# A two-layer recurrent trunk on one core: tokens halved in order instead of by parity

## The chip, the cores and the metric

The kernel runs on one core of a Trainium2 chip. Its engines are TensorE (matrix products, PE in the profile, with its weight loads shown apart as PEld), VectorE (DVE), ScalarE (ACT), GpSimd (POOL) and SyncE (SP), which here only issues transfers. The metric is the device time of one execution in microseconds; for the kernel before, the median of three runs is 1073.52 us.

## The reference

Two layers over 256 tokens of width 2048, all in fp32. The first layer projects the normed tokens into an HGRN2 mixer and an RG-LRU mixer, the second into an mLSTM mixer; each ends in an output projection added to the residual and in a gate that is a full 2048 x 2048 product:

```python
h = h + mix
pl = rmsnorm(p[i].astype(h.dtype) @ ple_w[i], ple_norm[i])
h = h + jax.nn.sigmoid(h @ ple_gate_w[i]) * pl
```

After the second layer a last RMSNorm is applied. What matters here is that each of the products takes all 256 tokens, that the output projections and gates produce rows by token (the residual is kept so), and that the next product needs these rows turned, features on the partitions.

## The kernel before

**Products.** Every operand is split into a rounded part and a remainder (hi and lo, type fp32r), and each product is made as hi·hi + hi·lo + lo·hi. `load_weights` (L116) brings 512 KB pieces through SyncE's queue into `raw` (five buffers), ACT casts them into `whi` (L130), VectorE subtracts into `wlo` (L131); both have four buffers, each a half of a quarter. `block` (L154) makes products with the weights stationary. `project_tok` (L190) makes those with the tokens stationary: for a block of 512 output columns it goes through four quarters `kq` of the contraction, in each through two halves of the tokens `hf`, and issues for each of four 128-row steps three products of 512 columns (L205, L206, L207): 96 products per column block, 24 per quarter. `quarter` (L1146) does the same with 256 columns for the last 512 output columns of the last gate.

**Which tokens form a half.** `tokens` (L187) picks the stationary operand. Where `even` is set, half 0 holds the even and half 1 the odd tokens: a step of two fp32 values over 128 columns. That is so in the output projections (`out_proj`, weights eo and oo), the gates (`ple_gate` with g0, and g1 with its last quarter) and the embeddings (`embed`). Elsewhere (ei, ez, ov, oog, oz) a half is 128 tokens in a row. The residual `hq` is loaded by parity (L882) and the result stored by parity (L1202).

**From rows to features.** After each column block c of an output projection or of g0, `to_features` (L353) turns 512 columns of the residual: VectorE transposes in blocks of 32 x 32 into w (L358), POOL writes w to DRAM (L476) and reads it back in four pieces as r (L479), and ACT and VectorE split r into the hi and lo of the next stationary operand. Without a gain (lanes fe after eo, fo after oo) ACT copies 256 columns (L370) and VectorE subtracts 256 (L371); with the gain of the next norm (lane fg after g0) `scaled_split` does both with a scale (L267, L268). In the lane fg a further step follows: `gate_sums` (L896), eight small products of r with the 16 columns of mLSTM's gates, with fp32 operands.

**Order.** Lanes are Python generators. `pump` (L74), called once in each quarter of a projection, takes every lane one `yield` further, behind the instructions last noted. `across` yields three times around the way through DRAM. `ready` (L376) lets the first projection of the next stage ask, at each quarter, for the two operands that this quarter needs; the last quarter needs the last column block of the stage before. Each engine takes its own queue in order; that order is fixed when the program is built, from the order of issue, `high_priority` and `issue_after`, and can differ from the order of the lines (the timeline shows two L205 behind each other where a lo part comes late).

**The norm ahead of the second layer.** `hidden_norm` (L909) sums squares, takes the reciprocal root per token, and spreads it along the free axis: a diagonal is built (L230), TensorE multiplies it with ones (L233), ACT copies the result (L251). Since its tokens are halved by parity and the following projections want halves in order, two more VectorE instructions (L917) pick the reordered values. ov's first eviction needs the values per token, the query and key projections the spread ones.

Of the kernel before, what the change touches and what calls it, by code (L numbers as in the profile page):

```python
# [19 lines left out]
P = 128  # L20
# [23 lines left out]
def trunk(ctx: ExitStack, tc: tile.TileContext, a, out):  # L44
# [142 lines left out]
    def tokens(x, k, hf, even):  # L187
        return x[:, k, hf::2] if even else x[:, k, hf * P:(hf + 1) * P]

    def project_tok(w, j, act, before=None, even=False):  # L190

        ps = [pm.tile([P, 512], F32, name="mm", tag="mm") for _ in range(2)]
        for kq in range(4):
            if before is not None:
                before(kq)
            parts = load_weights(w[4 * j + kq])
            for hf in range(2):
                for kk in range(4):
                    k = kq * 4 + kk
                    hi, lo = parts[kk // 2]  # L200
                    c = (kk % 2) * 512
                    ah, al, _ = act[k // 2]
                    xh, xl = (tokens(x, k % 2, hf, even) for x in (ah, al))
                    wh, wl = hi[:, c:c + 512], lo[:, c:c + 512]
                    te.matmul(ps[hf], xh, wh, start=(k == 0), stop=False)  # L205
                    te.matmul(ps[hf], xh, wl, start=False, stop=False)  # L206
                    last["pe"] = te.matmul(ps[hf], xl, wh, start=False, stop=(k == KT - 1)).ins  # L207
                if hf == 0:
                    pump()
        return ps  # L210
# [16 lines left out]
    def to_free(rt, even=False):  # L227

        dg = tp.tile([P, T], F32, name="dg", tag="dg", bufs=1)
        v.tensor_tensor(out=dg.rearrange("p (t h) -> p h t" if even else "p (h t) -> p h t", h=2), in0=ident.unsqueeze(1).to_broadcast([P, 2, P]),  # L230
                        in1=rt.unsqueeze(2).to_broadcast([P, 2, P]), op=ALU.mult)
        st = pst.tile([P, 512], F32, name="st", tag="st")
        te.matmul(st[:, 0:T], ones[:, 0:P], dg, start=True, stop=True)  # L233
        return st[:, 0:T]
# [13 lines left out]
    def free_copy(rt, name, even=False):  # L248
        ps = to_free(rt, even)
        rs = tp.tile([P, T], F32, name=name, tag="rsb")  # L250
        s.copy(rs, ps)  # L251
        return rs
# [45 lines left out]
    def embed(w, pact, tile_of, first=None):  # L298

        pls = []  # L300
        for b in range(2):
# [3 lines left out]
            for hi, lo in parts:  # L305
                halves = []
                for hf in range(2):
                    ps = pm.tile([P, 512], F32, name="mm", tag="mm")
                    for k in range(2):
                        xh, xl = (tokens(x, k, hf, True) for x in pact[0:2])  # L310
# [42 lines left out]
    def to_features(h, c, act, gain, name, more=None):  # L353

        w = room("w")
        w5 = w.rearrange("p (j c t h) -> p h c j t", j=4, c=4, h=2)
# [4 lines left out]
        r4 = r.rearrange("p (i c n) -> p c i n", i=4, c=4)  # L361
        for b in range(2):
            hi, lo, both = act_pair()
            for k in range(2):
                src = r4[:, 2 * b + k]
                hk, lk = (x[:, k].rearrange("p (i n) -> p i n", i=4) for x in (hi, lo))
                if gain:
                    scaled_split(src, gain, 4 * c + 2 * b + k, hk, lk)
                else:
                    s.copy(hk, src)  # L370
                    v.tensor_tensor(out=lk, in0=src, in1=hk.bitcast(F32), op=ALU.subtract)  # L371
            act[2 * c + b] = (hi, lo, both)
        if more is not None:
            more(c, r4)
# [8 lines left out]
    def out_proj(hq, w, y, lane):  # L383

        act = {}
        for c in range(4):
            ps = project_tok(w, c, y, even=True)
# [7 lines left out]
    def ple_gate(hq, w, act, pls, rp, hss, gain, lane, before, more):  # L395

        nxt = {}
        for c in range(4):
            ps = project_tok(w, c, act, None if c else before, even=True)
# [496 lines left out]
    def gate_sums(c, r4):  # L896
        for x in range(4):
            te.matmul(gps[32 * x:32 * x + 32, 0:T], wt[:, 4 * c + x], r4[:, x], start=(c == 0), stop=(c == 3))
# [10 lines left out]
    def hidden_norm():  # L909

        r = rsqrt_cols(total(hss0, 4))
        yield
        rs = free_copy(r, "hrs", even=True)
        rt, rth = (tp.tile([P, 2], F32, name=n, tag=n) for n in ("rt1", "rth"))
        for hf in range(2):
            sq = tp.tile([P, 512], F32, name="sq", tag="sq")[:, 0:P]
            v.scalar_tensor_tensor(sq, rs[:, hf * P:(hf + 1) * P], 1.0, ident, op0=ALU.mult, op1=ALU.mult,  # L917
                                   accum_out=rt[:, hf:hf + 1])
        v.tensor_scalar(rth, rt, 0.5, None, op0=ALU.mult)
        norm.update(rs=rs, rt=rt, rth=rth)  # L920
        yield
# [3 lines left out]
    with tc.tile_pool(name="m1", bufs=2) as m1:  # L925
# [212 lines left out]
        for g in range(3):  # L1138
            ps = project_tok(a["g1"], g, act, None if g else ready(act, "fo"), even=True)
# [6 lines left out]
        def quarter(g, order):  # L1146
            parts = load_weights(a["g1e"][2 * g]) + load_weights(a["g1e"][2 * g + 1])
            ps = [pm.tile([P, 512], F32, name="mm", tag="mm")[:, 0:T] for _ in range(2)]
            for n, (hf, kq) in enumerate(order):
                hi, lo = parts[kq]  # L1150
                for kk in range(4):
                    k = kq * 4 + kk
                    xh, xl = (tokens(x, k % 2, hf, True) for x in act[k // 2][0:2])
# [18 lines left out]
        for hf, ps in enumerate(quarter(1, [(hf, kq) for hf in range(2) for kq in range(4)])):  # L1172
# [15 lines left out]
            for g, c, n in ((1, 0, 256), (1, 256, 256), (0, 0, 512), (2, 0, 512), (3, 0, 512)):  # L1188
# [13 lines left out]
                x = on.dma_start(out=out.rearrange("(p h) f -> h p f", h=2)[hf, :, g * 512 + c:g * 512 + c + n], in_=o).ins  # L1202
# [119 lines left out]
```

## Time and profile before

| | us |
|---|---|
| median of three runs | 1073.52 |
| lowest and highest run | 1071.8, 1074.81 |
| the profiled execution | 1067.43 |
| its span, first to last instruction | 1065.7 |
| TensorE busy | 1049.1 |
| VectorE busy | 724.9 |
| ACT busy | 583.9 |

The stages with the tokens stationary lie in the profiled span at 308.7 to 397.6 us (eo), from there to some 492 us (g0), then ov up to 581 us, oog and oz up to 864 us, the second embedding, oo from 876.8 to 965.7 us, and g1 up to 1057 us with its last quarter from 1033.9 us. Rows of the profile name the line of the kernel, the engine, the operation and the tiles as out<-in; in a group's row the busy time and the mean duration of one follow, then the idle time ahead of them and what ended it. In the rows of a line stand the least, median and largest duration and the first and last start.

### The profile page before, as it was taken

What the parts mean: (1) busy time and instruction counts of PE and PEld (TensorE: products, weight loads), DVE (VectorE), ACT (ScalarE), POOL (GpSimd) and SP (SyncE); (2) the same over time, 40 slices, a digit from 0 to 9 for tenths busy, and PEclk for the clock granted to TensorE, in tenths of its full rate; (3) what the DMA queues carried; (4) which work ended last, traced back from release to release, by engine and by line L of the source; (5) the groups of instructions that cost most, each with busy time, mean ns of one, the idle gap of its engine ahead of it and who ended that gap; (6) DMA issues with size and microseconds to landing.
All of it is one profiled execution on the core that took longest, in us unless ns stands there. A gap on an engine that the chain in (4) does not pass through costs nothing.

```text
span 1065.7 us, 15134 instructions
## 1 busy us (share of the span) xinstructions
PE 1049.1 (98%) x5614; PEld 883.9 (83%) x5614; DVE 724.9 (68%) x1055; ACT 583.9 (55%) x877; POOL 143.4 (13%) x166
## 2 busy tenths in 40 slices
PE   7999999999999999999999999999999999999996
PEld 6888888888888888777888888888888888888886
DVE  6757797997876666657444887764457675656666
ACT  7675545869653444545445656654445575444543
POOL 0001332512204211111000000000001113311111
PEclk9999999999999999999999999999999999999998
DMA  9765554545868777766655544546557775877552
GB/s 358 276 215 189 173 166 151 178 159 191 262 249 257 238 230 219 237 218 228 201 187 196 173 159 159 168 159 197 198 185 233 250 260 184 274 241 234 193 178 80
DMA packets 63098, 221.21 MB, mean 208 GB/s; under 512 B 7728, under 2 KB 9008, under 8 KB 63024
## 3 DMA queue, kind: packets, MB, share of 16 engines
q1 hardware_dynamic: 55440, 196.64, 55.0%
q0 software_dynamic: 7152, 23.07, 7.2%
q8 instruction: 44, 0.72, 0.3%
q10 hardware_dynamic: 432, 0.52, 0.1%
q14 instruction: 30, 0.25, 0.1%
HBM read 209.20 MB, written 11.01 MB: 207 GB/s over the span
## 4 chain that ended last, share of the span: by engine, by line
PE 86%; issue 7%; DMA 4%; DVE 1%; POOL 1%; ACT 1%; ACTq 0%; POOLq 0%; DVEq 0%
PE mm L205 17%; PE mm L207 17%; PE mm L206 17%; PE mm L161 16%; PE mm L167 9%; DMA dfe<-w 2%; POOL r L479 1%; DMA dfg<-w 1%; PE mm L315 1%; PE mm L316 1%; PE mm L317 1%; PE mm L1157 1%; PE mm L1156 1%; PE mm L1155 1%; PE mx L792 1%
## 5 line engine op out<-in xcount | busy, mean ns | idle before, releaser
L131 DVE TENSOR_TENSOR wlo<-raw,whi 128x1024 fp32r<-128x1024 f32 (+1 forms) x363 | 443.4, 1237 | 261.0 <-ACT whi L130 227.3
L130 ACT CAST whi<-raw 128x1024 fp32r<-128x1024 f32 (+1 forms) x363 | 377.5, 1043 | 358.9 <-PE mm L207 262.3
L205 PE MATMUL mm<-whi,ahl 128*128 128x512 f32 x992 | 390.4, 394 | 0.0
L206 PE MATMUL mm<-wlo,ahl 128*128 128x512 f32 x992 | 388.5, 392 | 0.0
L207 PE MATMUL mm<-whi,ahl 128*128 128x512 f32 x992 | 387.9, 392 | 0.0
L205 PEld LDWEIGHTS mm<-whi,ahl 128*128 128x128 f32 x992 | 189.2, 191 | 39.5 <-ACT ahl L370 0.6
L207 PEld LDWEIGHTS mm<-whi,ahl 128*128 128x128 f32 x992 | 189.2, 191 | 39.4 <-issue 0.4
L206 PEld LDWEIGHTS mm<-wlo,ahl 128*128 128x128 f32 x992 | 189.3, 191 | 39.3 <-issue 0.8
L161 PE MATMUL mm<-ahl,whi 128*128 128x512 f32 x768 | 183.2, 391 | 0.0
L161 PEld LDWEIGHTS mm<-ahl,whi 128*128 128x128 f32 x768 | 141.4, 188 | 27.4
L167 PE MATMUL mm<-ahl,wlo 128*128 128x256 f32 x768 | 102.1, 286 | 0.0
L167 PEld LDWEIGHTS mm<-ahl,wlo 128*128 128x128 f32 x768 | 97.2, 191 | 3.6 <-issue 0.4
L476 POOL DMA_DIRECT2D ducn<-w x3 | 1.7, 561 | 332.7 <-DVE w L489 332.7
L173 ACT COPY sm<-mm 128x256 f32<-128x256 f32 x48 | 17.5, 365 | 30.9 <-PE mm L167 30.9
L938 DVE SCALAR_TENSOR_TENSOR qk<-mg,prm,qk 128x255 f32<-128x255 f32 (+2 forms) x48 | 21.1, 477 | 5.0 <-ACT qk L935 4.7
L174 DVE TENSOR_TENSOR mg<-mm,sm 128x256 f32<-128x256 f32 x48 | 19.9, 416 | 0.1
L315 PE MATMUL mm<-whi,ahl 128*128 128x512 f32 x32 | 14.1, 440 | 5.5 <-ACT whi L130 5.5
L1156 PE MATMUL mm<-wlo,ahl 128*128 128x256 f32 x64 | 18.1, 283 | 0.0
L1157 PE MATMUL mm<-whi,ahl 128*128 128x256 f32 x64 | 18.1, 283 | 0.0
L1155 PE MATMUL mm<-whi,ahl 128*128 128x256 f32 x64 | 18.1, 282 | 0.0
L184 DVE TENSOR_TENSOR mg<-mg,hrs 128x512 f32<-128x512 f32 (+1 forms) x25 | 17.1, 682 | 0.6
L358 DVE STREAM_TRANSPOSE w<-hq 128x512 f32<-128x512 f32 x24 | 17.0, 708 | 0.3
(288 smaller groups left out, 788.7 us busy)
## 6 DMA issues: line engine op xcount, KB each, us to landing
raw<-in_ew_dram SPq DMA_DIRECT2D x64, 512.0 KB, 4.2
raw<-in_g_dram SPq DMA_DIRECT2D x56, 512.0 KB, 4.4
raw<-in_eo_dram SPq DMA_DIRECT2D x32, 512.0 KB, 4.8
raw<-in_ov_dram SPq DMA_DIRECT2D x32, 512.0 KB, 3.8
raw<-in_oqk_dram SPq DMA_DIRECT2D x32, 512.0 KB, 4.0
raw<-in_oog_dram SPq DMA_DIRECT2D x32, 512.0 KB, 3.8
raw<-in_oz_dram SPq DMA_DIRECT2D x32, 512.0 KB, 3.9
raw<-in_oo_dram SPq DMA_DIRECT2D x32, 512.0 KB, 4.8
```

Source lines behind the costliest of these rows:

```text
L130: last["act"] = s.copy(h, r).ins
L131: last["dve"] = v.tensor_tensor(out=l, in0=r, in1=h.bitcast(F32), op=ALU.subtract).ins
L161: last["pe"] = te.matmul(ps, parts[k // 8][0][:, c:c + P], act[k // 2][2][:, (k % 2) * 512:(k % 2 + 1) * 512], start=(k == 0), stop=False).ins
L167: last["pe"] = te.matmul(ps[:, T:2 * T], parts[k // 8][1][:, c:c + P], act[k // 2][0][:, k % 2], start=False, stop=(k == KT - 1)).ins
L205: te.matmul(ps[hf], xh, wh, start=(k == 0), stop=False)
L206: te.matmul(ps[hf], xh, wl, start=False, stop=False)
L207: last["pe"] = te.matmul(ps[hf], xl, wh, start=False, stop=(k == KT - 1)).ins
L315: te.matmul(ps, xh, wh, start=(k == 0), stop=False)
L938: v.scalar_tensor_tensor(dst[:, sh:T], pi[:, 0:T - sh], pc("ccw", k * 16 + b), dst[:, sh:T], op0=ALU.mult, op1=ALU.add)
L1155: te.matmul(ps[hf], xh, wh, start=(k == 0), stop=False)
L1156: te.matmul(ps[hf], xh, wl, start=False, stop=False)
L1157: last["pe"] = te.matmul(ps[hf], xl, wh, start=False, stop=(k == KT - 1)).ins
```

## The change

Every half of the tokens is now 128 tokens in a row, and the parameter `even` is gone. The residual is loaded and the result stored in that order. The transposes write w in the order of halves. When r is split, the tokens are put in order: without a gain the copy and the subtractions go through a pattern with the halves outermost, the subtraction in two pieces of 128 columns; with a gain ACT writes scaled columns in order into a new tile x, and `split_act` makes hi (a copy of 512 columns) and lo (a subtraction of 512 columns) from it. The small gate products come two yields after the split. The norm ahead of the second layer uses `spread_norm`, one yield later at its start and one more ahead of the spreading, and the two reordering instructions are gone.

```diff
-    def tokens(x, k, hf, even):
-        return x[:, k, hf::2] if even else x[:, k, hf * P:(hf + 1) * P]
+    def tokens(x, k, hf):
+        return x[:, k, hf * P:(hf + 1) * P]
...
-        w5 = w.rearrange("p (j c t h) -> p h c j t", j=4, c=4, h=2)
+        w5 = w.rearrange("p (j c h t) -> p h c j t", j=4, c=4, h=2)
...
-        r4 = r.rearrange("p (i c n) -> p c i n", i=4, c=4)
+        r5 = r.rearrange("p (i c h t) -> p c h i t", i=4, c=4, h=2)
         for b in range(2):
-            hi, lo, both = act_pair()
-            for k in range(2):
-                src = r4[:, 2 * b + k]
-                hk, lk = (x[:, k].rearrange("p (i n) -> p i n", i=4) for x in (hi, lo))
-                if gain:
-                    scaled_split(src, gain, 4 * c + 2 * b + k, hk, lk)
-                else:
+            if gain:
+                x = tp.tile([P, 512], F32, name="xr", tag="hn", bufs=3)
+                for k in range(2):
+                    s.activation(x[:, k * T:(k + 1) * T].rearrange("p (h i t) -> p h i t", h=2, i=4), r5[:, 2 * b + k],
+                                 AF.Copy, scale=pc(gain, 4 * c + 2 * b + k))
+                act[2 * c + b] = split_act(x, "h")
+            else:
+                hi, lo, both = act_pair()
+                for k in range(2):
+                    src = r5[:, 2 * b + k]
+                    hk, lk = (x[:, k].rearrange("p (h i t) -> p h i t", h=2, i=4) for x in (hi, lo))
                     s.copy(hk, src)
-                    v.tensor_tensor(out=lk, in0=src, in1=hk.bitcast(F32), op=ALU.subtract)
-            act[2 * c + b] = (hi, lo, both)
+                    for hf in range(2):
+                        v.tensor_tensor(out=lk[:, hf], in0=src[:, hf], in1=hk[:, hf].bitcast(F32), op=ALU.subtract)
+                act[2 * c + b] = (hi, lo, both)
         if more is not None:
-            more(c, r4)
+            yield
+            yield
+            more(c, r5)
...
-    def spread_norm(rt):
+    def spread_norm(rt, lag=0):
         norm["rt"] = rt
         yield
+        if lag:
+            yield
         norm["rs"] = free_copy(norm["rt"], "hrs")
...
-            gp.dma_start(out=t, in_=a["x"].rearrange("(p h) f -> p h f", h=2)[:, :, i * 512:(i + 1) * 512])
+            gp.dma_start(out=t, in_=a["x"].rearrange("(h p) f -> p h f", h=2)[:, :, i * 512:(i + 1) * 512])
...
-    def gate_sums(c, r4):
+    def gate_sums(c, r5):
         for x in range(4):
-            te.matmul(gps[32 * x:32 * x + 32, 0:T], wt[:, 4 * c + x], r4[:, x], start=(c == 0), stop=(c == 3))
+            te.matmul(gps[32 * x:32 * x + 32, 0:T].rearrange("p (h i t) -> p h i t", h=2, i=4), wt[:, 4 * c + x],
+                      r5[:, x], start=(c == 0), stop=(c == 3))
...
-        r = rsqrt_cols(total(hss0, 4))
-        yield
-        rs = free_copy(r, "hrs", even=True)
-        rt, rth = (tp.tile([P, 2], F32, name=n, tag=n) for n in ("rt1", "rth"))
-        for hf in range(2):
-            sq = tp.tile([P, 512], F32, name="sq", tag="sq")[:, 0:P]
-            v.scalar_tensor_tensor(sq, rs[:, hf * P:(hf + 1) * P], 1.0, ident, op0=ALU.mult, op1=ALU.mult,
-                                   accum_out=rt[:, hf:hf + 1])
-        v.tensor_scalar(rth, rt, 0.5, None, op0=ALU.mult)
-        norm.update(rs=rs, rt=rt, rth=rth)
-        yield
+        yield
+        yield from spread_norm(rsqrt_cols(total(hss0, 4)), 1)
...
-                x = on.dma_start(out=out.rearrange("(p h) f -> h p f", h=2)[hf, :, g * 512 + c:g * 512 + c + n], in_=o).ins
+                x = on.dma_start(out=out[hf * P:(hf + 1) * P, g * 512 + c:g * 512 + c + n], in_=o).ins
```

More of the change, by code (lines that the diff above doesn't have):

```diff
@@ L202, in project_tok @@
                     ah, al, _ = act[k // 2]
-                    xh, xl = (tokens(x, k % 2, hf, even) for x in (ah, al))
+                    xh, xl = (tokens(x, k % 2, hf) for x in (ah, al))
                     wh, wl = hi[:, c:c + 512], lo[:, c:c + 512]
@@ L309, in embed @@
                     for k in range(2):
-                        xh, xl = (tokens(x, k, hf, True) for x in pact[0:2])
+                        xh, xl = (tokens(x, k, hf) for x in pact[0:2])
                         wh, wl = (x[:, k * 512:(k + 1) * 512] for x in (hi, lo))
@@ L398, in ple_gate @@
         for c in range(4):
[L399 removed]
+            ps = project_tok(w, c, act, None if c else before)
             for hf in range(2):
```

16 lines of the change are left out of this document (8 added, 8 removed).

## The prediction

> **What bounds the kernel now.** I read the page first (its busy table, the clock row and the chain that ended last), then single lines by stage, then TensorE's waits, then the timeline at the places where one projection hands over to the next.
>
> ```profile
> span 1065.7 us, 15134 instructions
> ...
> PE 1049.1 (98%) x5614; PEld 883.9 (83%) x5614; DVE 724.9 (68%) x1055; ACT 583.9 (55%) x877; POOL 143.4 (13%) x166
> ...
> PEclk9999999999999999999999999999999999999998
> ...
> PE 86%; issue 7%; DMA 4%; DVE 1%; POOL 1%; ACT 1%; ACTq 0%; POOLq 0%; DVEq 0%
> ```
>
> TensorE is busy for 98% of the span at the full clock and carries 86% of the chain. Nearly everything hangs on how far apart its products start and on the few places where it stands still. A product's duration (392 ns and so on) does not tell the first, because products overlap; the first and last start of a line's instructions in one stage do.
>
> ```profile
> L205 PE MATMUL mm<-whi,ahl x128: 392/394/394, 308.7 to 397.6; 128*128 128x512 f32 x128
> L205 PE MATMUL mm<-whi,ahl x128: 392/399/485, 876.8 to 965.7; 128*128 128x512 f32 x128
> L205 PE MATMUL mm<-whi,ahl x227: 389/389/584, 709.5 to 863.3; 128*128 128x512 f32 x114
> L206 PEld LDWEIGHTS mm<-wlo,ahl x128: 196/196/201, 876.8 to 965.7; 128*128 128x128 f32 x128
> L206 PEld LDWEIGHTS mm<-wlo,ahl x227: 187/188/188, 709.7 to 863.3; 128*128 128x128 f32 x114
> L1155 PE MATMUL mm<-whi,ahl x64: 278/283/283, 1033.9 to 1056.6; 128*128 128x256 f32 x64
> 67.60 1.91 PE mm L167 x16
> ```
>
> The first two rows are the two output projections, eo and oo, whose stationary operand takes every second token. The third is the end of oog and all of oz, which run the same lines with 128 tokens in a row. L205 starts once in three products, so eo spaces its products (397.6 - 308.7) / 127 / 3 = 233.3 ns apart, oo the same 233.3, and oog/oz (863.3 - 709.5) / 226 / 3 = 226.8 ns. The moving operand, the shape and the clock are the same; the stationary operand's step is what differs, and the loads themselves show it: 196 ns against 188. So a strided load costs 6.5 ns per product of 512 columns. At 256 columns it does not: the strided last quarter stands (1056.6 - 1033.9) / 63 / 3 = 120.1 ns apart, the contiguous L167 1.91 / 16 = 119.4.
>
> **The change part by part.**
>
> *A. Contiguous stationary operands.* Strided products of 512 columns: eo 4 x 96, g0 4 x 96, oo 4 x 96, the first three projections of g1 3 x 96, together 1440. 1440 x 6.5 ns = 9.4 us. The two embeddings have 48 each: the second gives 48 x 6.5 ns = 0.3 us, the first, which waits for its weights, at most as much; I take 0.2. The last quarter's 192 products gain nothing (120.1 against 119.4). A = 9.9 us; its bounds are 0, if the step is not the cause, and 192 x 0.7 ns more, 10.1 us.
>
> [...]
>
> *B. Two hand-overs where TensorE already waits for the token block.* g0 and the g1 stage need the last column block of the stage before in their last quarter, after 72 products.
>
> ```profile
> 407.47 2.18 POOL L479 DMA_DIRECT2D r<-dfe  x4 [4.89 <-DMA dfe<-w]
> 414.93 0.71 ACT L370 CAST ahl<-r 128x256 fp32r<-128x256 f32 x2
> 415.06 0.84 PE L205 MATMUL mm<-whi,ahl 128*128 128x512 f32 x2
> 415.74 0.39 PE L206 MATMUL mm<-wlo,ahl 128*128 128x512 f32 x1
> 983.24 0.94 PE L205 MATMUL mm<-whi,ahl 128*128 128x512 f32 x2
> 984.02 0.40 PE L206 MATMUL mm<-wlo,ahl 128*128 128x512 f32 x1
> ```
>
> Two products should take 0.47 us to the next start; they take 0.68 and 0.78, so TensorE is 0.2 and 0.3 us late there, waiting for ACT's copy of a block that has just come in. The way through DRAM starts at the end of the earlier stage and does not get faster, while TensorE arrives 72 x 6.5 ns = 0.47 us sooner. That part of A is handed back twice: B = -0.9 us. Without a copy's extra delay the bound is -0.9; if the copies or the four half-subtractions come late as well, 1 us more at each, -2.9.
>
> *C. Gate products two pumps later.*
>
> ```profile
> L898 PE MATMUL mx<-r,wg 128*32 128x256 f32 x32 | 2.6, 389 | 2.1 <-DMA r<-dfg 1.7 <-issue 0.5
> ```
>
> ```profile
> 463.41 0.51 ACT L267 ACTIVATE ahl<-r,prm 128x256 fp32r<-128x256 f32 x1 [2.19 <-DMA r<-dfg]
> ```
>
> TensorE takes its queue in order. In two of four column blocks of g0 the eight gate products L898 reach its head before the block r has landed, and the whole stream stands behind them for 1.7 and 0.5 us. The change issues them two pumps on, at least 24 large products later, so both waits go: C = +2.2 us. The products themselves, 2.6 us for all four blocks, stay. They now read r in runs of 32 instead of 64 values; no row here has such a moving operand, so the price lies between 0 and doubling, 2.6 us; I take 0, the nearest being the contiguous operands, since 32 values in a row are still a long run. C lies between -0.4 and +2.2.
>
> *D. The hand-over g0 to ov.* Here the stationary operand was contiguous after it and strided before it, but the block's split and the norm both change.
>
> ```profile
> 502.71 0.70 PE L233 MATMUL st<-dg,ones 128*128 128x256 f32 x2 [0.38 <-DVE dg L230]
> 508.91 1.05 ACT L130 CAST whi<-raw 128x1024 fp32r<-128x1024 f32 x1 [2.98 <-PE mm L207]
> 509.62 0.39 PE L206 MATMUL mm<-wlo,ahl 128*128 128x512 f32 x1
> 509.86 1.30 ACT L267 ACTIVATE ahl<-r,prm 128x256 fp32r<-128x256 f32 x3
> 509.93 0.64 PE L898 MATMUL mx<-r,wg 128*32 128x256 f32 x8
> 510.50 0.50 PE L207 MATMUL mm<-whi,ahl 128*128 128x512 f32 x1
> 511.07 1.04 ACT L130 CAST whi<-raw 128x1024 fp32r<-128x1024 f32 x1
> ```
>
> ```profile
> L145 ACT CAST ahl<-xr 128x512 fp32r<-128x512 f32 x10 | 6.1, 610 | 0.0
> L496 ACT ACTIVATE xr<-r,prm 128x256 f32<-128x256 f32 x12 | 5.4, 498 | 0.0
> ```
>
> Now ACT begins on the block at 509.86 and its first 256 columns serve the products after one instruction of 0.5 us, which the eight L898 (0.57 us) bridge. Afterwards the first product needs two scaled copies like L496, starting 0.4 us apart, and then a copy of both like L145: 0.4 + 0.5 + 0.61 = 1.5 us, ready at 511.4. TensorE, without the wait at L233 (0.4), without L233's own 0.35 and with L898 moved away, is done with what it has at 509.62 + 0.23 - 0.4 - 0.35 = 509.1. It waits 2.3 us, and 3.3 if the cast of 511.07 (1.04 us) is put between. What it lost here before is the 0.4 at L233 and some 0.2 around L898. D = -(2.3 - 0.6) = -1.7 us; from 0, if other products are put ahead, to -2.7.
>
> The norm moved by two pumps removes two short VectorE products and is late for nobody: the values per token are drained ahead of ov's first eviction, and those along the free axis are wanted by the query and key projections, four projections on. L233 and its wait on the diagonal may come back at the fourth pump: another 0.4, inside the bound.
>
> *E. ACT and VectorE instructions.*
>
> ```profile
> L371 DVE TENSOR_TENSOR ahl<-r,ahl 128x256 fp32r<-128x256 f32 x32 | 13.7, 453 | 0.5 <-ACT ahl L370 0.5
> L268 DVE SCALAR_TENSOR_TENSOR ahl<-r,prm,ahl 128x256 fp32r<-128x256 f32 x16 | 6.9, 481 | 1.5 <-ACT ahl L267 1.5
> L146 DVE TENSOR_TENSOR ahl<-xr,ahl 128x512 fp32r<-128x512 f32 x10 | 6.9, 688 | 2.7 <-ACT ahl L145 2.7
> ```
>
> ```profile
> 308.60:398.20 89.60, 89.60 (x386) 74.17 (x386) 59.31 (x71) 38.92 (x50) 24.09 (x26) 1.00 0.74 233
> 398.20:492.80 94.60, 92.47 (x410) 74.55 (x410) 60.34 (x73) 47.31 (x68) 10.98 (x20) 1.00 0.72 226
> ```
>
> In eo and oo 32 subtractions of 256 columns become 64 of 128. From 688 ns at 512 and 453 at 256 an estimate for 128 is 453 - (688 - 453) / 2 = 336 ns, so VectorE works 64 x 0.336 - 14.5 = 7.0 us more, at the worst 14.5 (no gain from halving). In g0 ACT gets eight copies, 8 x 0.61 = 4.9 us, and VectorE trades 16 x 481 for 8 x 688 ns, 2.2 us less. In the windows (busy TensorE, loads, VectorE, ACT, POOL; then clock, DMA share, GB/s) VectorE works 59.3 of 89.6 us in eo and ACT 47.3 of 94.6 in g0. The extra 3.5 and 4.9 us fit into 30 and 47 us idle beside TensorE: 0 on the path. Without that cover it would be up to 4.9 + 14.5 - 2.2 = 17.2 us, the second rival's ground. What is exposed at the hand-overs is in B and D.
>
> *F. At nothing:* the loads of the residual rows and the stores move the same pieces of 1 and 2 KB in other row order; the transposes write the same count with a pattern that feature_major has already; the way through DRAM is untouched. The stores are on the tail, so I leave 0.3 us to either side.
>
> *Sum.* 9.9 - 0.9 + 2.2 - 1.7 = 9.5 us. The profiled execution took 1067.43 us (its span 1065.7 and 1.7 around it), so 1057.9 of the same kind. The median of the runs, 1073.52, lies 6.1 us above the profiled execution; carrying that over gives **1064.0 us**, 0.9% faster. With every bound bad at once, keeping A at 9.4, 9.4 - 2.9 - 0.4 - 2.7 - 0.3 = 3.1 us (1070.4); with every one good, 10.1 - 0.9 + 2.2 + 0.3 = 11.7 (1061.8).
>
> **The rivals.**
>
> *The step of the stationary operand costs nothing* and 233.3 against 226.8 comes from something that goes with these stages. For it: at 256 columns no difference shows. Against it: the loads' 196 against 188 ns, and eo and oo, two far stages with different inputs, agree to the tenth. Then A and B vanish and C and D are left: +2.2 - 1.7 = 0.5 us, 1073.0. [...]
>
> *The row blocks hold ACT's queue: slower.* ACT too takes its queue in order. At 463.41 it stood 2.19 us for a block that had not landed, with the casts of the next weights queued behind it. The change makes such a block longer on ACT in g0 and on VectorE in eo and oo, and TensorE arrives earlier. If the cover is gone, each of the 12 blocks costs such a wait: 12 x 2.19 = 26.3, less 9.5, so 16.8 us slower, 1090.3. It decides from where a cast is later than the weight buffers reach: four halves of 12 products, so three halves ahead, 36 x 0.227 = 8.2 us. Against it: TensorE's waits hold a single one on a cast, at the start of the program:
>
> ```profile
> PE mm L315 <- ACT whi L130: 5.5, 1, 5.5
> ```
>
> *The way through DRAM falls behind.* With a stream 3% denser (226.8 for 233.3), the weight loads crowd the small transfers, which share 0.74 of the DMA engines' time in eo already. If each of the three hand-overs waits 1.7 us longer still, as long as L898 waited, 5.1 us go: 9.5 - 5.1 = 4.4, 1069.1. For it: B's rows, where TensorE is already late. Against it: the loads only start when TensorE frees a buffer, so their share grows by 3% at most.
>
> **How the numbers follow.** My sum 0.80, its own range 1060 to 1069; no cost of the step 0.08; ACT's queue 0.07; the way through DRAM 0.05. The runs of before differ by 3 us among themselves, so 0.3%, 3.2 us, is what can be told from no change. The first and the last are faster by more than that: 0.85. The second is within it: 0.08. ACT's queue is slower: 0.07. The range 1059 to 1070 adds the bounds and some 1.5 us for the runs' own scatter; it holds the first case and the last and leaves out the others.
>
> **What would show it.** Right: eo and oo show first and last starts of L205 some 86.4 us apart (127 x 3 x 226.8 ns) and loads near 188 ns; L898 has no wait on r; TensorE's idle time gathers in three places, the last quarter of g0's first project, of g1's first and above all of ov's first, there waiting for ACT's copy of the split. The quarter stays at 120 ns. Wrong: 233 ns with contiguous loads ends A; waits of products on casts spread through g0 would show ACT's queue; waits over 2 us at all three hand-overs, with r landing late, the DRAM way.

## The result and the profile after

The changed kernel takes 1083.53 us (median of four runs, 1080.3 to 1087.65) against 1072.66 for the kernel before beside it (four runs, 1070.1 to 1074.81). The ratio is 1.0104, interval [1.0058, 1.0150]: it became 1% slower, where 1064.0 us was forecast. The profiled execution took 1081.47 us, 14.0 more than the one of before.

From the page of the changed kernel, the rows that answer to those of before:

```profile
span 1079.6 us, 15164 instructions
...
PE 1047.7 (97%) x5614; PEld 878.7 (81%) x5614; DVE 724.8 (67%) x1075; ACT 586.5 (54%) x885; POOL 140.5 (13%) x166
...
PEclk9999999999999998999899999999999999999999
...
PE 46%; DMA 2%; issue 2%; ACT 1%; POOL 1%; DVE 0%; ACTq 0%; POOLq 0%
...
L376 DVE TENSOR_TENSOR ahl<-r,ahl 128x128 fp32r<-128x128 f32 x64 | 15.0, 288 | 19.3 <-ACT ahl L374 19.3
```

TensorE is busy for 1.4 us less and the span is 13.9 us longer, so its idle time grew by 15.3 us. Closer products alone would have taken 9.7 us from the busy time (9.4 in A, 0.3 for the second embedding); by that estimate some 8 us of the busy time are a loss too, and the clock row has two slices under nine tenths of full speed. The single line L205 for the stage eo (weight load, then product: least, median and largest ns, first and last start; its window opens two of these products late and takes in two of g0):

```profile
L205 PEld LDWEIGHTS mm<-whi,ahl x128: 187/188/188, 309.0 to 396.3; 128*128 128x128 f32 x128
L205 PE MATMUL mm<-whi,ahl x128: 388/389/395, 309.2 to 396.5; 128*128 128x512 f32 x128
```

The loads take 188 ns; in the kernel before they take 193 in eo and 196 in oo. First and last start of the products lie 87.3 us apart; less one stop of 0.9 us that is 86.4, as forecast: products stand 226.8 ns apart. The gain of the closer spacing is there. What ate it stands in the waits of TensorE, and of ACT, of the changed kernel (us in total, times, longest):

```profile
PE mm L205 <- ACT ahl L374: 9.1, 2, 5.9
PE mm L205 <- ACT whi L130: 6.1, 2, 4.2
...
PE mm L206 <- DVE wlo L131: 2.6, 4, 0.8
```

```profile
ACT ahl L374 <- DMA r<-dfe: 20.4, 4, 7.3
...
ACT xr L366 <- DMA r<-dfg: 11.6, 3, 5.4
```

And ACT's waits on row blocks in the kernel before:

```profile
ACT ahl L267 <- DMA r<-dfg: 2.9, 2, 2.2
...
ACT ahl L370 <- DMA r<-dfe: 2.1, 2, 1.3
```

ACT's waits for the four blocks of fe grew from 2.1 to 20.4 us. The timeline of the changed kernel at the third of them shows who stands behind (start, us, engine, line; in brackets the idle time and what ended it):

```profile
389.22 1.05 ACT L130 CAST whi<-raw 128x1024 fp32r<-128x1024 f32 x1 [3.02 <-PE mm L207]
...
397.55 0.71 ACT L374 CAST ahl<-r 128x256 fp32r<-128x256 f32 x2 [7.28 <-DMA r<-dfe]
397.98 0.70 DVE L376 TENSOR_TENSOR ahl<-r,ahl 128x128 fp32r<-128x128 f32 x3 [6.46 <-ACT ahl L374]
398.16 1.04 ACT L130 CAST whi<-raw 128x1024 fp32r<-128x1024 f32 x1
...
399.23 1.22 DVE L131 TENSOR_TENSOR wlo<-raw,whi 128x1024 fp32r<-128x1024 f32 x1 [0.56 <-ACT whi L130]
...
399.25 0.49 PE L205 MATMUL mm<-whi,ahl 128*128 128x512 f32 x1 [1.91 <-ACT whi L130]
...
400.58 0.68 DVE L397 TENSOR_TENSOR hq<-mm,hq 128x512 f32<-128x512 f32 x1
...
401.98 0.70 DVE L358 STREAM_TRANSPOSE w<-hq 128x512 f32<-128x512 f32 x1
```

At 390.27 ACT reaches the copy of block r and stands there for 7.28 us. Behind it, in its queue, is the cast of the next weights; it runs at 398.16, and TensorE, out of weights, starts again at 399.25. VectorE stands for the same block (6.46 us). So the residual sum (L397) and the transposes (L358) of the next column block come late too: its projection ended at 395.8, its transposes start at 401.98. That block is then written late, lands late, and ACT waits for it again. POOL's issues of those writes in the changed kernel, and then in the kernel before:

```profile
334.28 0.60 POOL L485 DMA_DIRECT2D dfe<-w  x1 [2.00 <-DVE w L358]
...
357.03 0.60 POOL L485 DMA_DIRECT2D dfe<-w  x1 [8.09 <-DVE w L358]
...
381.44 0.56 POOL L485 DMA_DIRECT2D dfe<-w  x1 [15.60 <-DVE w L358]
...
406.44 0.56 POOL L485 DMA_DIRECT2D dfe<-w  x1 [16.19 <-DVE w L358]
```

```profile
335.18 0.60 POOL L476 DMA_DIRECT2D dfe<-w  x1 [3.74 <-DVE w L358]
...
357.64 0.60 POOL L476 DMA_DIRECT2D dfe<-w  x1 [7.40 <-DVE w L358]
...
379.98 0.56 POOL L476 DMA_DIRECT2D dfe<-w  x1 [13.81 <-DVE w L358]
...
402.02 0.56 POOL L476 DMA_DIRECT2D dfe<-w  x1 [14.32 <-DVE w L358]
```

Before, the writes are 22.5, 22.3 and 22.0 us apart, the pace of the products (96 x 233.3 ns = 22.4). After, they are 22.8, 24.4 and 25.0 apart where the products allow 21.8. It is a loop around DRAM: late block, waiting ACT, late cast and late transposes, later block. Set against the end of each projection (from the starts of the products), ACT waits 2.26, 4.91 and 7.28 us for the first three blocks and the next writes are 1.83, 4.48 and 6.82 us later than the 3.8 us that they take undisturbed (in oo of the kernel before): each wait is passed on all but some 0.44 us. The way through DRAM adds to it. From the issue of the write to the last landing it took the four blocks 13.7, 15.4, 16.0 and 16.1 us, against 12.6, 13.7, 13.2 and 12.8 before; no run shows why.

TensorE's longest stop also cost time after it ended. The timeline at eo to g0 in the changed kernel, and the granted clock there (the last three numbers of a window are clock, DMA share and GB/s):

```profile
416.70 0.44 PE L205 MATMUL mm<-whi,ahl 128*128 128x512 f32 x1
423.05 0.79 PE L205 MATMUL mm<-whi,ahl 128*128 128x512 f32 x1 [5.90 <-ACT ahl L374]
423.64 0.63 PE L206 MATMUL mm<-wlo,ahl 128*128 128x512 f32 x1
424.07 0.63 PE L205 MATMUL mm<-whi,ahl 128*128 128x512 f32 x1
...
427.39 0.39 PE L206 MATMUL mm<-wlo,ahl 128*128 128x512 f32 x1
```

```profile
423.00:427.00 4.00, 3.95 (x9) 3.14 (x10) 2.93 (x9) 1.86 (x4) 0.00 (x0) 0.50 0.12 28
427.00:440.00 13.00, 13.00 (x58) 10.74 (x57) 8.58 (x10) 6.31 (x10) 0.56 (x1) 0.99 0.52 175
```

After 5.9 us of standing the granted clock (1.00 is full speed) is 0.50 for 4 us and products start 0.43 us apart instead of 0.227. From 416.70 to 427.39 eleven products take 10.7 us instead of 2.5: 8.2 lost. By the same count the other places lose 0.9 (374.5), 4.4 (397), 8.4 (514 to 526, g0 to ov) and 4.9 (994, oo to g1): 26.8 in all. Before lost 3.3 at these places and in L898. 26.8 - 3.3 = 23.5, less the 9.7 that the spacing gives, is 13.8 of the 14.0 us. Shorter stops had a tail as well: near 400 us, after two of 1.9 and 0.8 us close together, the granted clock was 0.62 from 399 to 403 us, with products 0.43 us apart. After the single stop of 0.6 us at 375 it stayed at 1.00.

A ratio below leaves out executions over 1.5% above a kernel's fastest, while the median beside it is over all of them, so the two can differ for kernels that scatter widely.

### The profile page after: what moved, and what is told of

It reads as the page before. It is cut to its first block, busy times and chain, and to the rows that moved or that the text cites. A ratio compares the mean times of both kernels' runs of the same rounds, so it can differ in the third digit from the quotient of the medians.

```text
span 1079.6 us, 15164 instructions
## 1 busy us (share of the span) xinstructions
PE 1047.7 (97%) x5614; PEld 878.7 (81%) x5614; DVE 724.8 (67%) x1075; ACT 586.5 (54%) x885; POOL 140.5 (13%) x166
## 4 chain that ended last, share of the span: by engine, by line
PE 46%; DMA 2%; issue 2%; ACT 1%; POOL 1%; DVE 0%; ACTq 0%; POOLq 0%
PE mm L205 11%; PE mm L206 11%; PE mm L207 11%; PE mm L161 5%; PE mm L167 3%; DMA r<-dfg 1%; PE mm L1158 1%; PE mm L1157 1%; PE mm L1156 1%; PE nu L1038 1%; DMA r<-ducn 1%; DMA r<-dfo 1%; POOL r L488 1%; DMA ducn<-w 0%; ACT whi L130 0%
## 5 line engine op out<-in xcount | busy, mean ns | idle before, releaser
L130 ACT CAST whi<-raw 128x1024 fp32r<-128x1024 f32 (+1 forms) x363 | 376.6, 1043 | 328.3 <-PE mm L207 238.9
L205 PE MATMUL mm<-whi,ahl 128*128 128x512 f32 x992 | 391.8, 395 | 15.2 <-ACT ahl L374 9.1
L205 PEld LDWEIGHTS mm<-whi,ahl 128*128 128x128 f32 x992 | 188.1, 190 | 57.7 <-ACT ahl L374 9.7
L376 DVE TENSOR_TENSOR ahl<-r,ahl 128x128 fp32r<-128x128 f32 x64 | 15.0, 288 | 19.3 <-ACT ahl L374 19.3
L374 ACT CAST ahl<-r 128x256 fp32r<-128x256 f32 x32 | 11.4, 402 | 26.4 <-DMA r<-dfe 20.4
L939 DVE SCALAR_TENSOR_TENSOR qk<-mg,prm,qk 128x255 f32<-128x255 f32 (+2 forms) x48 | 21.1, 478 | 5.0 <-ACT qk L936 4.7
L315 PE MATMUL mm<-whi,ahl 128*128 128x512 f32 x32 | 13.8, 431 | 5.5 <-ACT whi L130 5.2
```

What stands on the lines that cost most here:

```text
L130: last["act"] = s.copy(h, r).ins
L939: v.scalar_tensor_tensor(dst[:, sh:T], pi[:, 0:T - sh], pc("ccw", k * 16 + b), dst[:, sh:T], op0=ALU.mult, op1=ALU.add)
```

## The experiments

In all kernels called "tokens mixed up" the order of the tokens within the halves is not consistent, so the computed rows are mixed; sizes and counts are unchanged.

### Spacing and the rest, apart

e1 is the kernel before with `tokens` always returning `x[:, k, hf * P:(hf + 1) * P]`; e2 is the changed kernel with `x[:, k, hf::2]` in eo, g0, oo and g1.

> The kernel before with one edit: every stationary operand takes 128 tokens in a row. Residual rows, splits, gate products and the norm stay as they were, so tokens get mixed up in the result; the instructions and their order on every engine are those of before. Theory P: products 226.8 ns apart, but ACT waits 2 to 7 us at many of the L370/L267 blocks, TensorE waits on casts and operands for over 10 us, time 1072 to 1085. Theory S (the changed splits and their place in the queues cost the time): the gain of the pace comes through, 1062 to 1066, ACT waits as before. Theory R: faster than before by 5 to 10 us when compared on one chip.

> The changed kernel with one edit: the stationary operands of the output projections, gates and embeddings take every second column again, so tokens get mixed up in the result; splits, gate products and norm stay as changed. Theory P: products 233.3 ns apart, ACT waits at the row blocks back under 2.5 us each, and with the gate products' waits gone 1069 to 1074. Theory S: slower than the changed kernel by the lost pace, 1088 to 1094. Theory R: same as theory S.

e1: 1070.13 us (1059.78 to 1081.9, 10 runs), ratio 0.9979 [0.9935, 1.0022]. e2: 1083.82 (1073.37 to 1086.68, 4 runs), 1.0103 [1.0030, 1.0175]. Closer products alone bring nothing in the median; the rest of the change costs 1% even at the old spacing (four runs). Neither lies where an expectation put it: e1 is below the 1072 to 1085 of theory P, although the waits that it names are there, and e2 is above theory P's 1069 to 1074 and below theory S's 1088 to 1094. The kernel before, profiled once more beside these (1076.64 us), has ACT wait only 0.2 us for fe's blocks, so it is not that the transfers had become slower for every kernel. In e1, with no other edit, the waits of TensorE and of ACT show the loop:

```profile
PE mm L205 <- ACT ahl L370: 7.9, 2, 7.1
```

```profile
ACT ahl L370 <- DMA r<-dfe: 15.1, 4, 7.2
```

So closer spacing is enough to start it. In this execution its gain comes through in oo and g1, where the loop does not run (153.6 us for the two, 157.2 in the trace of before); eo and g0 together take 188.7 us instead of 184.0.

### The wait taken out of the loop

If ACT's place in the loop is the cause, it must go when ACT copies a block so late that it always has landed. In e3 the changed kernel splits the first three blocks of each lane three pumps later (the fourth is needed at once); e4 does that to the kernel before; e5 is e4 with operands in a row, tokens mixed up.

```diff
-        yield from across(w, r, f"d{name}{c}")
+        yield from across(w, r, f"d{name}{c}", 3 if c < 3 else 0)
...
-    def across(w, r, name):
+    def across(w, r, name, late=0):
...
-        for _ in range(3):
+        for _ in range(3 + late):
```

> The changed kernel with the split of the first three row blocks of each stage three pumps later, so that it stands three to four casts further back in ACT's queue; the fourth block is forced by its user as before. Theory P: the ACT waits at nine of twelve blocks go, the hand-overs keep theirs (about 14 us in the first profile of the changed kernel, slow clock included), 1070 to 1076. Theory S: as the changed kernel, 1080 to 1086. Theory R: between, since waits on slow transfers go where there is time to wait: 1074 to 1080.

> The kernel before with one edit: the splits of the first three row blocks of each stage three pumps later (the gate products of g0 with them). Stationary operands keep their step of two. Loop theory (a block that ACT must wait for delays the weight casts behind it, these delay the next block's turning, so that the next wait is longer; the late split takes ACT out of it): little to gain at this pace, as the first profile showed waits of 0 to 2.2 us; the gate products' waits of 2.2 us go, and rare slow runs get rarer: 1066 to 1070. Theory that the late place alone makes the gain of the earlier late kernel: 1058 to 1062.

> The kernel before with two edits: tokens in a row in every stationary operand (rows stay by parity, so tokens get mixed up in the result) and the splits of the first three row blocks three pumps later. The splits themselves are those of before. Loop theory: the pace comes through, 9.4 us less than the kernel before with the late splits alone, 1057 to 1061, the same as the changed kernel with late splits within 2 us. Theory that the changed split work costs time by itself (more ACT copies, subtractions of 128 columns): 3 us or more faster than the changed kernel with late splits.

| kernel | median us (runs) | ratio |
|---|---|---|
| e3, changed, late splits | 1060.72 (10) | 0.9914 [0.9876, 0.9951] |
| e4, before, late splits | 1071.25 (10) | 1.0010 [0.9974, 1.0045] |
| e5, before, in a row, late splits | 1061.81 (10) | 0.9915 [0.9877, 0.9952] |

So the loss hangs on when the blocks are taken up, and not on the amount of work. The same changed code, with its splits issued later, turns from 1.0% slower into 0.9% faster, lower than any of the three theories had it (1070 at best). From e4 to e5, where only the spacing differs, 9.4 us go (each scatters by 13 us), against term A less B's 0.94, 9.0; both lie up to 1.3 us above the ranges that the loop theory gave them. From e5 to e3 the whole remaining change (splits, gate products, norm) moves 1.1 us, less than the runs scatter, and the ratios are the same. And e4 says that the lateness itself brings nothing to the kernel before in total. The edit moves VectorE's subtractions along with ACT's copies, so what each of the two queues adds is not told apart; and a late split also covers a longer way through DRAM. With late splits that way is not longer, though, at the same spacing: 11.0 to 13.8 us for fe's blocks in e3, 11.8 to 13.6 in e6 below (e5 has one block of 15.2 beside three of 11.3 to 12.7).

### The best version

feature_major sends blocks through the same `across` in the stage oz (lane ducn), untouched by the change; in e3 ACT still waits there. e6 is e3 with this lane late as well:

```diff
-        yield from across(w, r, f"du{gain}{first}")
+        yield from across(w, r, f"du{gain}{first}", 3 if gain == "cn" else 0)
```

> The changed kernel with late splits in the stages eo, g0 and oo as before, and in oz too, where feature_major turns mLSTM's rows. Loop theory: in oz ACT waited 3.5, 6.4 and 3.6 us in the profile of the kernel with late splits, and the stage took 160 us in place of 155; that goes: 1055 to 1060, and the runs lie closer together. If these waits cost nothing: as the kernel with late splits, 1058 to 1064.

1057.6 us (1056.58 to 1058.33, 4 runs), ratio 0.9880 [0.9847, 0.9914]: faster than both kernels, and the four runs lie 1.8 us apart, where the ten of e3 lie 12.4 apart. Its page, TensorE's waits, and POOL's issues of the fe writes:

```profile
span 1056.5 us, 15170 instructions
...
PE 87%; issue 5%; DMA 4%; ACT 2%; POOL 1%; DVE 1%; ACTq 0%; POOLq 0%; DVEq 0%
```

```profile
PE mm L206 <- DVE wlo L131: 1.5, 2, 0.8
PE mm L205 <- ACT ahl L374: 0.9, 2, 0.6
```

```profile
333.29 0.60 POOL L485 DMA_DIRECT2D dfe<-w  x1 [3.94 <-DVE w L358]
...
355.96 0.60 POOL L485 DMA_DIRECT2D dfe<-w  x1 [10.33 <-DVE w L358]
...
377.71 0.56 POOL L485 DMA_DIRECT2D dfe<-w  x1 [13.24 <-DVE w L358]
...
399.47 0.56 POOL L485 DMA_DIRECT2D dfe<-w  x1 [14.13 <-DVE w L358]
```

The writes are now 22.7, 21.8 and 21.8 us apart, the pace of the products, and the hand-overs eo to g0 and oo to g1 keep the waits that B named: 0.8 and 0.6 us by the starts of the products, against 0.2 + 0.47 and 0.3 + 0.47.

Counted from a stage's first product to the next stage's first, in one execution each (us; oog takes 91.7 in all):

| stage | before | changed | e1 | e3 | e6 |
|---|---|---|---|---|---|
| eo | 89.6 | 88.0 | 87.7 | 87.8 | 88.2 |
| g0 | 94.4 | 101.4 | 101.0 | 89.0 | 89.6 |
| ov to oog | 193.4 | 201.9 | 193.5 | 194.5 | 194.9 |
| oz, second embedding | 99.1 | 99.4 | 98.8 | 106.9 | 99.6 |
| oo | 89.7 | 87.2 | 87.2 | 87.2 | 87.2 |
| g1 to its last quarter | 67.5 | 70.4 | 66.4 | 66.7 | 66.0 |

The change loses in g0, from ov to oog and in g1, and with late splits these losses are gone. The stage oz varies by itself wherever its splits are not late: it took 106.3 us in the other execution of the kernel before, so a difference of some us between totals need not come from an edit.

### Which part feeds the loop

e8 is the kernel before with the two yields ahead of `more(c, r4)`: step C alone.

> The kernel before with one edit: the small gate products of g0 two pumps later. Everything else, the step of two included, stays. My step C: their waits of 2.2 us on TensorE go and nothing comes in their place, 1067 to 1069. Loop theory: TensorE's wait at the gate products kept it in step with the row blocks; without it ACT's waits at the blocks of g0 grow from one to the next (2, 3, 5 us) and end as a wait of TensorE at the first projection after g0: no gain or a loss, 1070 to 1077, with writes of the blocks from 5.1 us to over 7 us behind the end of the projection.

1070.98 us (10 runs), ratio 0.9999 [0.9958, 1.0040]. The waits of L898 are gone from its trace, the total is the same, and ACT's waits in g0 do not grow: the expectation of growth missed. C's 2.2 us would be a ratio of 0.998, inside the interval. The one trace has them: g0 takes 91.3 us instead of 94.4 and ov to oog 194.3 instead of 193.4, together 2.2 us less; oz, which the edit does not touch, took 104.8 us in this execution and hides it.

Then the changed kernel with one part undone at a time: e9 the split of fe and fo (one subtraction of 256 columns), e10 that of fg (`scaled_split`), e11 both, all with tokens mixed up; e7 the two yields.

```diff
-                    src = r5[:, 2 * b + k]
+                    src = r4[:, 2 * b + k]
...
-                    for hf in range(2):
-                        v.tensor_tensor(out=lk[:, hf], in0=src[:, hf], in1=hk[:, hf].bitcast(F32), op=ALU.subtract)
+                    v.tensor_tensor(out=lk, in0=src, in1=hk.bitcast(F32), op=ALU.subtract)
```

> The changed kernel with the split of the lanes fe and fo as before: ACT's copy and one subtraction of 256 columns in the order in which r lies. The two halves of the tokens are mixed up against the residual, with the same sizes; the lane fg, the gate products and the norm stay changed. Open is which part of the changed code feeds the row of late blocks that costs 1% even at the old spacing. Theory 1: it is the subtraction in two pieces in fe and fo, which puts work between VectorE's lo parts of the weights and its transposes. Then this kernel lands near the kernel before with its operands in a row, 1070 +- 4 us, and ACT's waits on r in fe fall to 0.5, 2.8, 4.5 and 7.2 us or below. Theory 2: it is the lane fg (three ACT instructions for a pair of columns instead of two): 1081 to 1085 us, fe's waits as in the changed kernel, up to 7.3 us. Theory 3: neither, but the later norm or the later gate products: 1081 to 1085 us here and in the next two runs.

> The changed kernel with the split of the lane fg as before: scaled copy and scaled subtraction of 256 columns, in the order in which r lies. The halves of the tokens of ov's, the query's and the key's operands are mixed up, with the same sizes; fe and fo, the gate products and the norm stay changed. Theory 1 (the subtractions of fe and fo): 1081 to 1085 us, fe's waits up to 7 us. Theory 2 (the lane fg): 1070 +- 4 us, with ACT's waits on r in fg at 2 us or below, and ov's first product no longer late. Both in part: the two runs lie between, near 1076 each.

> Both of the last two edits together: the changed kernel with the splits of all three lanes as before, tokens mixed up as there. What stays of the change are the operands in a row, the later gate products, the norm by the common path and the loads and stores. Theories 1 and 2: 1070 +- 4 us, no difference from the kernel before with its operands in a row (1070.1). Theory 3 (the norm or the later gate products): 1081 to 1085 us. If e9 and e10 both stay high and this one is low, the two splits feed the same row of late blocks and either is enough.

> The changed kernel without the two extra yields: the small gate products follow the split at once, as before. If they held TensorE in step with the blocks (TensorE waits for r itself, so ACT's wait on r costs nothing more and does not grow), ACT's waits on r in the lane fg shrink from 2.4, 3.8, 5.4 to below 2 us, the gate products show waits on r of 2 us or more, and the time falls to 1078 or below. If they only move the wait: 1083 +- 3 us. By the prediction's term C it would be 2.2 us slower, 1086.

Four more complete the table: e12 the changed kernel again; e13 e11 with the gate products at once; e14 e1 with the gate products later; e15 e2 with the gate products at once.

> The changed kernel once more, for more executions beside the runs below. Expected 1083 +- 3 us with a spread of some 15 us. If it comes out near 1075, the four executions known so far were high by chance and the differences between e7, e9, e10 and e11 say nothing of the parts.

> The changed kernel with the splits of before in all lanes (tokens mixed up as there) and the gate products at once: operands in a row, the norm by the common path, the loads and stores remain. If the later gate products feed the late blocks, this equals the kernel before with operands in a row, 1070 +- 3 us. If the norm's place feeds them, it stays at e11's 1081.8 +- 4.

> The kernel before with all stationary operands in a row and the gate products two pumps later (tokens mixed up, norm and splits as before). If the later gate products feed the late blocks at the closer spacing, since TensorE no longer stops for r itself: 1080 +- 4 us. If it is the norm: 1070 +- 3.

> The changed kernel with step-two stationary operands (tokens mixed up) and the gate products at once; the splits and the norm stay changed. If every part takes some of the slack of the row blocks and none is enough alone: 1072 +- 4 us, against 1083.8 with the later gate products. If the changed splits are enough alone at the old spacing: 1080 or more.

| kernel | spacing | splits | gate products | median us (range, runs) | ratio |
|---|---|---|---|---|---|
| changed | closer | changed | later | 1083.53 (1080.3-1087.7, 4) | 1.0104 [1.0058, 1.0150] |
| e12 | closer | changed | later | 1082.01 (1080.4-1097.6, 6) | 1.0100 [1.0045, 1.0155] |
| e9 | closer | fg changed | later | 1080.44 (1072.7-1101.4, 10) | 1.0071 [1.0032, 1.0109] |
| e10 | closer | fe, fo changed | later | 1081.79 (1069.0-1095.4, 10) | 1.0050 [1.0001, 1.0098] |
| e11 | closer | before | later | 1081.75 (1063.8-1092.4, 10) | 1.0020 [0.9967, 1.0073] |
| e14, norm of before | closer | before | later | 1078.39 (1058.1-1087.7, 12) | 0.9953 [0.9905, 1.0001] |
| e7 | closer | changed | at once | 1075.10 (1070.1-1083.2, 10) | 1.0040 [1.0003, 1.0078] |
| e13 | closer | before | at once | 1079.01 (1061.7-1092.2, 12) | 0.9994 [0.9949, 1.0040] |
| e1, norm of before | closer | before | at once | 1070.13 (1059.8-1081.9, 10) | 0.9979 [0.9935, 1.0022] |
| e2 | old | changed | later | 1083.82 (1073.4-1086.7, 4) | 1.0103 [1.0030, 1.0175] |
| e15 | old | changed | at once | 1076.15 (1064.9-1083.5, 12) | 1.0016 [0.9981, 1.0051] |

The kernel before beside them stood at 1070.4 to 1072.7 us. No single part is the culprit: no undoing brings the 0.991 of e3 back. By their medians, undoing the splits does not help (e9, e10 and e11 lie within 1 us of theory 3's range). But none of the ten executions of the changed kernel (with e12) is below 1080 us, and thirteen of the thirty of e9, e10 and e11 are, so the splits seem to make the good executions rare. Issuing the gate products later raises the median by 7 to 8 us in three pairs (e7 to e12, e1 to e14, e15 to e2) and by 2.7 from e13 to e11. The runs of a pair stood beside different runs of the kernel before, though, their intervals overlap, and from e1 to e14 the ratio even falls. The stages tell more. From ov to oog the four kernels with closer products or changed splits and the gate products at once (e1, e7, e13, e15) took 192.7 to 193.5 us, as before the change; the changed kernel, e2, e9, e10, e11, e12 and e14, with them later, took 195.1 to 204.1. At the old spacing with the old splits (e8) it is 194.3. The trace shows what the gate products did. ACT's waits in g0 in e7, gate products at once:

```profile
447.75 1.31 ACT L366 ACTIVATE xr<-r,prm 128x256 f32<-128x256 f32 x3 [1.73 <-DMA r<-dfg]
...
473.29 1.31 ACT L366 ACTIVATE xr<-r,prm 128x256 f32<-128x256 f32 x3 [1.28 <-DMA r<-dfg]
...
496.48 1.31 ACT L366 ACTIVATE xr<-r,prm 128x256 f32<-128x256 f32 x3
```

And in e12, gate products later:

```profile
451.83 1.31 ACT L366 ACTIVATE xr<-r,prm 128x256 f32<-128x256 f32 x3 [5.50 <-DMA r<-dfg]
...
476.37 0.51 ACT L366 ACTIVATE xr<-r,prm 128x256 f32<-128x256 f32 x1 [7.40 <-DMA r<-dfg]
...
500.95 0.51 ACT L366 ACTIVATE xr<-r,prm 128x256 f32<-128x256 f32 x1 [4.73 <-DMA r<-dfg]
```

With the gate products at once TensorE stands for r together with ACT, and the next block has that time to catch up: the waits die away. In e13, where ACT's waits in g0 are 4.0, 2.4, 0.9 and 0.4 us, the gate products (L905 there) stand 3.8, 1.9 and 0.5 us:

```profile
PE mx L905 <- DMA r<-dfg: 6.2, 3, 3.8
```

Without that stop, waits of this size keep on through g0 into ov: 5.5, 7.4, 4.7 and 5.7 us in e12, 4.2, 6.9, 7.1 and 5.2 in e9. Where they start small they can stay so (0.1, 0.9, 0.5 and 1.3 us in e11). One execution each is known; e15 (1.8 us, then none) decays as e13 does. Whether the norm's new place has a share (e13 against e1) stays open: the two were measured beside different runs and both scatter by 20 us or more. e15's median (1076.15) lies at the edge of what was expected if no part is enough alone, and e13's (1079.01) inside what was expected of the norm.

## Why the prediction was wrong

**A, the spacing,** was right in size: 86.4 us in eo, 188 ns loads, and 9.4 us from e4 to e5. The rival that the step costs nothing falls: no trace shows the step for free at 512 columns, and the products of eo, 233.3 ns apart with it, stand 226.8 apart without.

**B, two hand-overs,** was right where no loop runs (0.8 and 0.6 us in e6). But it looked for the lost slack at two places only. TensorE arrives 72 x 6.5 ns = 0.47 us sooner at every one of the twelve blocks, and ACT with it: at fe's first two it is free 16.2 us after the end of the projection, 16.65 before. In e1, without any of the other edits, that is enough to lose A's gain.

**C, the gate products,** was right for the kernel before, as far as one trace of e8 shows (2.2 us less in g0 and ov). It failed beside the rest of the change: there the waits would have held TensorE to the pace of the blocks, and without them the stretch from ov to oog took 201.9 us instead of 193.0 (e7).

**D, g0 to ov:** 2.3 us of waiting forecast, 8.4 lost in the profiled execution, since the last block of fg arrived with the loop's lateness; the cast put ahead of the products, which D had as its bad bound, is there too (4.2 us behind L130). Where no loop runs the term fits: some 1.5 us more from ov to oog in e6, against 1.7.

**E is the step that failed:** "The extra 3.5 and 4.9 us fit into 30 and 47 us idle beside TensorE: 0 on the path". The amount of work was not the fault: the 128-column subtraction took 288 ns (336 estimated), and with late splits the changed code costs nothing (e3 against e5). The fault is to take ACT's idle time in a window for cover. The idle time is there, but ACT's next instruction stood behind a wait for r, and that wait had no slack left: in the trace of before ACT already waited up to 1.3 us for blocks of fe and 2.2 for fg. What had to be compared was when a block lands and when ACT comes to it. By the starts of the products before, fe's blocks land 16.6 to 17.9 us after the end of their projection, and where ACT waits for one it is free at 16.65. Nothing was left to take, and a wait that is passed on to the next block adds up: in the changed kernel the four blocks land 18.3, 21.1, 24.3 and 26.7 us after it.

**The second rival** (ACT's queue held by row blocks) was in the main the right mechanism, at a chance of 0.07; VectorE's queue belongs to it. Its price was twelve independent waits of 2.19 us; in fact the waits feed each other within a lane and start afresh at each stage, and TensorE pays for a part of them, mainly at hand-overs, with 2 to 4 us of products 0.43 us apart after them (granted clock 0.50 from 423 to 427 us). Its counter-argument, a single wait of a product on a cast in the trace of before, showed only that the loop had not started. The third rival (the way through DRAM) has a share: of the 6.0 us by which fe's third block lands later than its first, 3.6 are a later write and 2.4 a longer way. But its reason, denser weight loads, does not hold by itself, since in e3 and e6, as dense, the way is as short as before. The median read of fe took 6.8 us from issue to landing in the changed kernel and 5.5 before, as the transfer rows have it, and 5.5 in e6:

```profile
r<-dfe POOLq DMA_DIRECT2D x16, 128.0 KB, 6.8
```

```profile
r<-dfe POOLq DMA_DIRECT2D x16, 128.0 KB, 5.5
```

The sum of 9.5 us fits a kernel in which no loop runs: the profiled execution of e6 took 1058.33 us, 9.1 less than that of the kernel before. That e3 is 9.8 us below the kernel before is partly luck, since in oz it still waits. The bounds of the range held no case in which a gain of pace starts a loop.

## What to carry to other kernels

Where a result goes out and comes back for a later stage, follow one item round: when does it land, and when does the engine that takes it up reach that place in its queue? Here the two differed by less than the round trip varied (fe's blocks landed 16.6 to 17.9 us after their projection, and ACT was there at 16.65, in the changed kernel at 16.2), so a faster stream turned into waits, and idle time elsewhere on ACT was no cover. Issue the taking-up later, as far as its first user allows; a wait on the fast engine that looks like a loss may be what keeps the others in step (here the four traces with it and the seven without), so take it away only after that.

## What the runs showed of the hardware

- A stationary operand with a step of two fp32 values costs 6.5 ns per product of 512 columns (233.3 against 226.8) and nothing that shows at 256 (120.0 ns before and after).
- In the changed kernel, after TensorE stood for 2 to 6 us, its products of 512 columns started 0.43 us apart instead of 0.227 for 2 to 4 us; after the longest stop, of 5.9 us, the granted clock was 0.50 for 4 us.
- The kernel before has the same loop in code that the change does not touch: in another execution of it (1076.64 us) ACT waited 9.6 us for the three blocks of ducn in oz, which in the execution shown before the prediction wait for nothing. With all splits late the spread from run to run, 13 us for the kernel before beside it (25 runs), shrank to 1.8 us (four runs).
